# Tiles, banks, sums, masks and first loads of a two-layer network kernel on one Trainium2 core

## The chip, the core and the metric

The kernel runs on one core of a Trainium2 chip. The metric is the device time of one execution in microseconds. Before the change three runs took 2057.19, 2058.51 and 2059.92 us, so the median is 2058.51.

## The reference

The network has two residual layers on a stream of 512 tokens and 2048 features, all in fp32.

- Layer A (HGRN2): an RMS norm, a product with a 2048 x 8192 matrix that gives queries, forget gates, values and an output gate for 16 heads, a gated linear recurrence over the tokens, a norm per head, the gate, a product with a 2048 x 2048 matrix, and the sum with the stream.
- Layer B (forgetting attention): keys, values and forget sums from the stream after layer A, queries and gate, attention with a decay per head, the gate, and again a product with a 2048 x 2048 matrix and the sum.

```python
...
    proj = h @ w_in
...
    o = o.reshape(B, T, D_MODEL) * jax.nn.silu(gate.astype(jnp.float32))
    return x + (o.astype(x.dtype) @ w_out)
```

## The kernel before

Everything is kept with features on the 128 partitions and the 512 tokens along the free axis, so the stream is 16 tiles ("slices", kt) of 128 x 512. An fp32 product is made of three products in a rounded format: each operand is split into a high part h and a low part l, and h·xh, h·xl and l·xh are summed in PSUM. The split of a weight tile is a cast on ScalarE (L435, or L147 where a norm's weight is multiplied in) and a subtraction on VectorE (L436, L148). Weights are read by the SP queue, 512 KB at a time into two buffers `wr` (`Chunks.load`, L190).

An ordinary group (`group`) makes four output tiles in the four PSUM banks `gm0` to `gm3`: 16 slices of 12 matmuls each, 128 x 512 (L237 to L239, with the tokens on the other side L233 to L235). The first one of the program reads the input `x` too, 256 KB a slice (`fetch_x`, L456); `load_x` splits it (L469, L470), feeds the norm's sum of squares (`Norm.add`: ScalarE squares into `z`, GpSimd adds, L350), and does one step of setup for each slice, among them the ten masks of layer A (`mask`: a memset, two selections, a cast, L514 to L523).

The program runs through four phases: layer A ("a"), its output projection ("oa"), layer B ("b"), its output projection ("ob"). Each phase has a pool of its own, which is closed when the next one opens; `mt` takes a tile from the phase's pool, `nt` from a persistent one. In "oa" and "ob" (`out_product`) the first ordinary group makes four of the 16 output tiles, with the splits of its inputs (`y_split`) and the preparation of the sums of inputs (`quick_prep`, tile `tm`) between its slices. Then six seven-product groups (`quick_groups`, `quick`) make two output tiles each, by a scheme of 7 products for 8: 168 matmuls of 128 x 256 (L290 to L292), with sums of weight parts on VectorE (`w_sums`, L156 to L158, tile `wm`) and their split (`w_split_quick`). These groups take the banks `gm` and `mx` in turn; `quick_sum` (L299 to L309) evacuates them. The evacuation of the last of the six in "oa" is deferred (`last_a`) into the third slice of the first group of "b", whose inputs are split by `x1_split`. `x1_done` stores a finished tile of the stream and adds its squares to the next norm. At the end of "a" the gate of the last four heads is made by `gate_evac` (VectorE L381, ScalarE L367 to L384, VectorE L370 and L387) before the inputs of "oa" are complete.

The order of the instructions on each engine is set by a scheduler that simulates the program; each engine then works through its own row of instructions in that order and waits for semaphores. The weights of the split were, before, in tiles of the phase's pool:

```python
    def w_tiles(shape):

        n = 2 if cur["quick"] else 3
        return mt("wh", shape, n, F32R), mt("wl", shape, n, F32R)
```

## Time and profile before

| | |
|---|---|
| runs (us) | 2057.19, 2058.51, 2059.92 |
| profiled execution: time, span (us) | 2057.41, 2055.4 |
| mean granted TensorE clock | 0.987 |
| busy: TensorE, VectorE, ScalarE, GpSimd (us) | 1986.9, 1585.9, 1133.1, 305.6 |
| bytes moved | 195.01 MB |

The profiled execution's own time is 2.0 us over its span. The share of busy time is an average over the stages; where an engine waits is read from the timeline, which gives after each group of instructions the idle time before it and what ended it. A matmul's duration is longer than the distance to the next one's start, since matmuls are pipelined. The granted clock is given as a share of full speed, where 1.0 stands for 2.4 GHz.

### The profile page before, as it was taken

How to read it: one execution, taken by the hardware profiler on the slowest of the kernel's cores; microseconds unless marked ns; L12 is line 12 of the kernel's file. 1: busy time of each engine (PE TensorE's matmuls, PEld its weight loads, DVE VectorE, ACT ScalarE, POOL GpSimd, SP SyncE). 2: the span in 40 equal slices, each digit the busy share in tenths (PEclk: the TensorE clock that was granted, in tenths of full speed). 3: DMA queues.
4: the chain of work that ended last, by engine and by line, in shares of the span. 5: the costliest groups of instructions: out<-in, count | busy, mean ns of one | idle time of the engine just before them, and what ended most of it. 6: DMA issues, size and time to landing. Idle time of an engine off the chain costs nothing.

```text
span 2055.4 us, 28924 instructions
## 1 busy us (share of the span) xinstructions
PE 1986.9 (97%) x10202; PEld 1696.2 (83%) x10202; DVE 1585.9 (77%) x3250; ACT 1133.1 (55%) x2312; POOL 305.6 (15%) x404
## 2 busy tenths in 40 slices
PE   7999999999999999889999999999999999997998
PEld 5888888888888888779987888888888888885898
DVE  8778977989799889688984667666766666687787
ACT  5656655656566466644453555554555556564333
POOL 7303210313133031121110000010001000011000
PEclk9999999999999999989999999999999999998999
DMA  5222222222222222234433233223222322222453
GB/s 170 88 83 74 71 84 81 75 80 83 74 81 72 73 83 73 81 96 151 159 115 95 91 93 97 88 79 101 93 88 92 92 90 90 90 86 72 135 173 103
DMA packets 61408, 195.01 MB, mean 95 GB/s; under 512 B 7872, under 2 KB 8000, under 8 KB 61264
## 3 DMA queue, kind: packets, MB, share of 16 engines
q1 hardware_dynamic: 61120, 193.17, 30.0%
q8 instruction: 80, 1.31, 0.3%
q14 instruction: 64, 0.52, 0.1%
q10 hardware_dynamic: 144, 0.01, 0.0%
HBM read 184.73 MB, written 8.42 MB: 94 GB/s over the span
## 4 chain that ended last, share of the span: by engine, by line
PE 74%; DVE 13%; DMA 4%; issue 3%; ACT 3%; POOL 2%; SPq 0%; DVEq 0%; ACTq 0%; POOLq 0%
PE gm L237 16%; PE gm L239 16%; PE gm L238 16%; PE gm L234 5%; PE gm L233 5%; PE gm L235 5%; DVE wl L436 3%; DMA wr<-in_wa_q 2%; DMA wr<-in_wb_q 2%; PE mx L583 1%; PE mx L581 1%; PE mx L582 1%; DVE ml L436 1%; PE mx L430 1%; PE mx L431 1%
## 5 line engine op out<-in xcount | busy, mean ns | idle before, releaser
L237 PE MATMUL gm<-xh,wh 128*128 128x512 f32 x1664 | 654.2, 393 | 37.6 <-ACT wh L435 36.5
L238 PE MATMUL gm<-xl,wh 128*128 128x512 f32 x1664 | 653.5, 393 | 0.0
L239 PE MATMUL gm<-xh,wl 128*128 128x512 f32 x1664 | 605.8, 393 | 6.0 <-DVE wl L436 5.5
L237 PEld LDWEIGHTS gm<-xh,wh 128*128 128x128 f32 x1664 | 314.7, 189 | 102.9 <-ACT wh L435 37.6
L239 PEld LDWEIGHTS gm<-xh,wl 128*128 128x128 f32 x1664 | 312.4, 189 | 70.3 <-DVE wl L436 7.2
L238 PEld LDWEIGHTS gm<-xl,wh 128*128 128x128 f32 x1664 | 314.7, 189 | 63.5
L435 ACT CAST wh<-wr 128x512 fp32r<-128x512 f32 (+1 forms) x336 | 217.4, 650 | 217.6 <-PE gm L238 114.8
L436 DVE TENSOR_TENSOR wl<-wr,wh 128x512 fp32r<-128x512 f32 (+1 forms) x336 | 257.5, 770 | 75.5 <-ACT wh L435 60.7
L148 DVE SCALAR_TENSOR_TENSOR wl<-wr,v_b_norm_w,wh 128x256 fp32r<-128x256 f32 (+1 forms) x192 | 114.1, 596 | 137.5 <-ACT wh L147 129.2
L147 ACT ACTIVATE wh<-wr,v_b_norm_w 128x256 fp32r<-128x256 f32 (+1 forms) x192 | 111.8, 585 | 185.2 <-PE gm L238 144.0
L234 PE MATMUL gm<-wl,xh 128*128 128x512 f32 x512 | 201.5, 394 | 0.4 <-DVE wl L436 0.4
L235 PE MATMUL gm<-wh,xl 128*128 128x512 f32 x512 | 200.0, 392 | 0.0
L233 PE MATMUL gm<-wh,xh 128*128 128x512 f32 x512 | 183.6, 392 | 0.3 <-DVE q L547 0.2
L147 ACT ACTIVATE wh<-wr,v_kv_norm_w 128x256 fp32r<-128x256 f32 (+1 forms) x192 | 110.3, 574 | 59.4 <-PE gm L235 43.1
L148 DVE SCALAR_TENSOR_TENSOR wl<-wr,v_kv_norm_w,wh 128x256 fp32r<-128x256 f32 (+1 forms) x192 | 112.2, 586 | 35.8 <-ACT wh L147 35.3
L934 POOL TENSOR_SCALAR_AFFINE_SELECT s<-s 128x128 f32<-128x128 f32 x64 | 27.3, 427 | 647.7 <-DVE s L933 647.0
L576 DVE COPY_PREDICATED at<-m,mx 128x128 f32<-128x128 uint8 (+3 forms) x448 | 106.8, 297 | 11.2 <-PE mx L583 10.7
L233 PEld LDWEIGHTS gm<-wh,xh 128*128 128x128 f32 x512 | 96.0, 188 | 20.4 <-ACT wh L435 0.5
L234 PEld LDWEIGHTS gm<-wl,xh 128*128 128x128 f32 x512 | 96.3, 188 | 19.5 <-DVE wl L436 1.0
L235 PEld LDWEIGHTS gm<-wh,xl 128*128 128x128 f32 x512 | 96.3, 188 | 18.4
L435 ACT CAST kh<-k 128x512 fp32r<-128x512 f32 (+1 forms) x96 | 56.5, 588 | 52.3 <-PE mx L582 19.2
L385 POOL TENSOR_TENSOR z<-z,t 128x512 f32<-128x512 f32 x32 | 46.4, 1460 | 230.3 <-ACT t L384 230.3
(217 smaller groups left out, 3890.4 us busy)
## 6 DMA issues: line engine op xcount, KB each, us to landing
wr<-in_wa_qf SPq DMA_DIRECT2D x64, 512.0 KB, 3.5
wr<-in_wb_qk SPq DMA_DIRECT2D x64, 512.0 KB, 3.5
wr<-in_wa_v SPq DMA_DIRECT2D x32, 512.0 KB, 3.5
wr<-in_wa_g SPq DMA_DIRECT2D x32, 512.0 KB, 3.5
wr<-in_wb_v SPq DMA_DIRECT2D x32, 512.0 KB, 3.5
wr<-in_wb_g SPq DMA_DIRECT2D x32, 512.0 KB, 3.5
wr<-in_wa_q SPq DMA_DIRECT2D x24, 512.0 KB, 3.6
wr<-in_wb_q SPq DMA_DIRECT2D x24, 512.0 KB, 3.6
```

Of the source, the lines that this page charges most:

```text
L147: S.activation(h[:, c], r[:, c], AF.Copy, scale=w[:, kt : kt + 1])
L148: V.scalar_tensor_tensor(l[:, c], r[:, c], w[:, kt : kt + 1], rd(h)[:, c], op0=ALU.mult, op1=ALU.subtract)
L233: PE.matmul(banks[j], xh, h, start=f, stop=False)
L234: PE.matmul(banks[j], xh, l, start=False, stop=False)
L235: PE.matmul(banks[j], xl, h, start=False, stop=e)
L237: PE.matmul(banks[j], h[:, c], Xh[kt], start=f, stop=False)
L238: PE.matmul(banks[j], h[:, c], Xl[kt], start=False, stop=False)
L239: PE.matmul(banks[j], l[:, c], Xh[kt], start=False, stop=e)
L385: G.tensor_mul(z, z, l)
L435: S.copy(h, src)
L436: return V.tensor_sub(l, src, rd(h))
L576: V.copy_predicated(out, mv, data)
```

## The change

1. Weight tiles: `w_tiles` is gone. An ordinary split takes three buffers `wh`, `wl` of the persistent pool in all phases; a seven-product split takes two buffers `w7h`, `w7l` of the phase's pool. The scratch tile `t` has three buffers in the output projections and four elsewhere, and the tile of `quick_prep` is one of the two buffers `wm`.
2. Banks: the seven-product groups 0, 2 and 4 take `mx`, the groups 1, 3 and 5 `gm`; before it was the other way round.
3. Norm sums: `Norm.add` adds on VectorE instead of GpSimd, and the call for layer B's norm is moved from `x1_done` (when a tile of the stream is finished) to `x1_split` (when the next phase splits it).
4. Masks: all ten are made in one tile at the start, with one memset, twenty selections and one cast.
5. First loads: the first two weight loads are halved, and each half follows an input tile.

```diff
--- before.py
+++ after.py
@@ -65,7 +65,7 @@
         return t.bitcast(F32)
 
     def tmp():
-        return mt("t", (P, T), 4)
+        return mt("t", (P, T), cur["t"])
 
     def bank():
         return nt("mx", (P, T), 4, pool=ps)
@@ -78,7 +78,7 @@
         if cur:
             cur["ctx"].close()
         cur["ctx"] = c = ExitStack()
-        cur["quick"] = name[0] == "o"
+        cur["t"] = 3 if name[0] == "o" else 4
         cur["sb"] = c.enter_context(tc.tile_pool(name=f"sb{name}", bufs=1, reuse_waits="tile"))
 
     phase("a")
@@ -131,13 +131,8 @@
     load_vec("a_norm_w", S)
 
 
-    def w_tiles(shape):
-
-        n = 2 if cur["quick"] else 3
-        return mt("wh", shape, n, F32R), mt("wl", shape, n, F32R)
-
     def w_split(r, kt, scales):
-        h, l = w_tiles((P, T))
+        h, l = nt("wh", (P, T), 3, F32R), nt("wl", (P, T), 3, F32R)
         if scales is None:
             split(r, h, l)
         else:
@@ -160,7 +155,7 @@
 
     def w_split_quick(r, m):
 
-        h, l = w_tiles((P, 2, 7, P))
+        h, l = mt("w7h", (P, 2, 7, P), 2, F32R), mt("w7l", (P, 2, 7, P), 2, F32R)
         split(r[:, :, 1:4, :], h[:, :, 0:3, :], l[:, :, 0:3, :])
         split(m, h[:, :, 3:7, :], l[:, :, 3:7, :])
         return [(h[:, i, :, :], l[:, i, :, :]) for i in range(2)]
@@ -181,13 +176,18 @@
             for k in range(KT // 4):
                 self.todo.append((ap[k], True, None, 0))
 
-        def load(self):
+        def load(self, between=None):
 
             if not self.todo:
                 return
             ap, quick, scales, kt = self.todo.pop(0)
             r = nt("wr", (P, 2 * T), 2)
-            nc.sync.dma_start(r, ap)
+            if between:
+                nc.sync.dma_start(r[:, :T], ap[:, :T])
+                between()
+                nc.sync.dma_start(r[:, T:], ap[:, T:])
+            else:
+                nc.sync.dma_start(r, ap)
             if quick:
                 self.raw.append((lambda r=r.rearrange("p (a b c) -> p a b c", a=2, c=P): w_split_quick(r, w_sums(r)), 2))
             else:
@@ -250,7 +250,7 @@
 
         k1, k2 = 2 * p, 2 * p + 1
         b11, b12, b21, b22 = y[k1][:, :TN], y[k1][:, TN:], y[k2][:, :TN], y[k2][:, TN:]
-        m = mt("tm", (P, 4, TN), 1)
+        m = mt("wm", (P, 4, TN), 2)
         V.tensor_sub(m[:, 0, :], b12, b11)
         G.tensor_sub(m[:, 2, :], b12, b22)
         V.tensor_sub(m[:, 1, :], b22, m[:, 0, :])
@@ -313,7 +313,7 @@
         for u in range(6):
             k = 4 + 2 * u
             r = [residual(k), residual(k + 1)]
-            banks = [nt(f"gm{j}", (P, T), 1, pool=ps) if u % 2 == 0 else bank() for j in range(4)]
+            banks = [nt(f"gm{j}", (P, T), 1, pool=ps) if u % 2 else bank() for j in range(4)]
             end = quick(banks, prep, lambda *p, k=k, r=r: evac(k, r, p), hold and u == 5)
             if u < 5:
                 end()
@@ -347,7 +347,7 @@
             else:
                 q = nt("z", (P, T), 4)
                 S.activation(q, x, AF.Square)
-                G.tensor_add(self.acc, self.acc, q)
+                V.tensor_add(self.acc, self.acc, q)
             self.n += 1
 
         def finish(self):
@@ -455,11 +455,10 @@
             xs.append(nt(f"y{kt}", (P, T), 1))
             nc.sync.dma_start(xs[kt], io["x"][kt])
 
-    for kt in range(2):
-        fetch_x()
-    wts.load()
     fetch_x()
+    wts.load(fetch_x)
     fetch_x()
+    wts.load(fetch_x)
 
     def load_x(kt):
         fetch_x()
@@ -503,15 +502,19 @@
     setup.append(lower_bounds)
 
 
-    def mask(name, m, d, q0):
-        n = 4 - q0
-        g = P // (4 * m)
-        u = const(name, (P, g * n * m), U8)
-
-        def make():
-            f = tmp()
-            fv = f[:, : g * n * m].rearrange("p (g q r) -> p g q r", g=g, q=n)
-            G.memset(f[:, : g * n * m], 1.0)
+    masks = {}
+    levels = [(1, 0, 0), *((m, d, d) for m in (1, 4, 16) for d in (1, 2, 3))]
+    sizes = [P // 4 * (4 - q0) for _, _, q0 in levels]
+    all_masks = const("masks", (P, sum(sizes)), U8)
+
+    def make_masks():
+        f = mt("e", (P, 4 * T))[:, : sum(sizes)]
+        G.memset(f, 1.0)
+        at = 0
+        for (m, d, q0), size in zip(levels, sizes):
+            n = 4 - q0
+            g = P // (4 * m)
+            fv = f[:, at : at + size].rearrange("p (g q r) -> p g q r", g=g, q=n)
             G.affine_select(
                 out=fv, in_=fv, pattern=[[-4 * m, g], [-m, n], [0, m]], compare_op=ALU.is_ge,
                 fill=0.0, base=m * (d - q0), channel_multiplier=1,
@@ -520,15 +523,11 @@
                 out=fv, in_=fv, pattern=[[4 * m, g], [m, n], [0, m]], compare_op=ALU.is_ge,
                 fill=0.0, base=m * (q0 - d) + m - 1, channel_multiplier=-1,
             )
-            V.tensor_copy(u, f[:, : g * n * m])
-
-        setup.append(make)
-        return u
-
-    masks = {(1, 0): mask("m1_0", 1, 0, 0)}
-    for m in (1, 4, 16):
-        for d in (1, 2, 3):
-            masks[m, d] = mask(f"m{m}_{d}", m, d, d)
+            masks[m, d] = all_masks[:, at : at + size]
+            at += size
+        V.tensor_copy(all_masks, f)
+
+    make_masks()
     ats = [const(f"at{i}", (P, NW, P)) for i in range(2)]
     setup.append(lambda: [V.memset(t, 0.0) for t in ats])
 
@@ -804,7 +803,6 @@
 
     def x1_done(kt):
         nc.sync.dma_start(x1_d[kt], X1[kt])
-        norm1.add(X1[kt])
 
     def out_a_evac():
         res = [res_a(j) for j in range(4)]
@@ -851,6 +849,7 @@
             forget_weights()
         h, l = new_x(kt)
         split(X1[kt], h, l)
+        norm1.add(X1[kt])
         X1[kt] = None
         if kt == KT - 1:
             norm1.finish()
@@ -859,7 +858,7 @@
     wfs = mt("wfs", (P, KT, 48), 1, F32R)
 
     def forget_weights():
-        wf = mt("t", (P, KT, H), 4)
+        wf = mt("t", (P, KT, H), cur["t"])
         nc.sync.dma_start(wf, io["wb_f"])
         V.memset(wfs.bitcast(F32), 0.0)
         V.tensor_mul(wf, wf, view(nk, 0, [[1, KT], [0, H]]))
```

Three places show how the order moves. In all rows a line of the changed kernel has its own line numbers (L143 is the old L148, L186 and L188 are the halves of a load, L532 the old L533).

The SP queue at the start of the program; `y` is an input tile, `wr` a weight buffer. Before:

```order
L456 DMA y_3_84<-in_x 128x512
L456 DMA y_4_86<-in_x 128x512
L190 DMA wr_88<-in_wa_qf 128x1024
L456 DMA y_6_90<-in_x 128x512
L456 DMA y_7_92<-in_x 128x512
L128 DMA v_lb<-in_lb 128x16
```

And now:

```order
L456 DMA y_3_84<-in_x 128x512
L186 DMA wr_86<-in_wa_qf 128x512
L456 DMA y_5_88<-in_x 128x512
L188 DMA wr_86<-in_wa_qf 128x512
L456 DMA y_6_91<-in_x 128x512
L186 DMA wr_93<-in_wa_qf 128x512
L456 DMA y_8_95<-in_x 128x512
L188 DMA wr_93<-in_wa_qf 128x512
L128 DMA v_lb<-in_lb 128x16
```

The first weights come in halves of 128 x 512, the first of them behind one input tile, and the second weight load comes ahead of the small vectors.

ScalarE at the end of phase "a" and the start of "oa"; L367 to L384 are the gate of the last heads, `xh` are input splits, `wh` weight splits. Before, from the last steps of the gate:

```order
L384 ACTIVATE t_9250<-t_9250 128x512
L384 ACTIVATE t_9263<-t_9263 128x512
L384 ACTIVATE t_9276<-t_9276 128x512
L435 CAST xh_1878_9641<-y_1426_7294 128x512
L435 CAST xh_1882_9661<-y_1502_7684 128x512
L435 CAST xh_1890_9694<-y_1619_8290 128x512
L435 CAST wh_9323<-wr_9214 128x512
L435 CAST wh_9327<-wr_9214 128x512
```

And now, from the last split of the group before:

```order
L435 CAST wh_9291<-wr_9148 128x512
L435 CAST wh_9295<-wr_9148 128x512
L367 ACTIVATE t_9205<-z_9203 128x512
L435 CAST wh_9326<-wr_9182 128x512
L367 ACTIVATE t_9218<-z_9216 128x512
L368 ACTIVATE t_9205<-t_9205 128x512
L367 ACTIVATE t_9231<-z_9229 128x512
L368 ACTIVATE t_9218<-t_9218 128x512
L367 ACTIVATE t_9244<-z_9242 128x512
L369 ACTIVATE t_9205<-t_9205 128x512
L368 ACTIVATE t_9231<-t_9231 128x512
```

The first three weight splits of the projection (`wh_9291`, `wh_9295`, `wh_9326`), which came behind the gate, stand ahead of it and in its first steps.

VectorE at the end of the last seven-product group of "oa" and the start of "b"; L436 with `xl` are the next phase's input splits, L350 the norm's sums, L300 to L309 the deferred evacuation. Before, from the last weight split of the projection:

```order
L436 TENSOR_TENSOR wl_11142<-wm_11137,wh_11141 128x2x512
L436 TENSOR_TENSOR xl_2144_11534<-y_2047_10977,xh_2143_11533 128x512
L436 TENSOR_TENSOR xl_2148_11556<-y_2048_10978,xh_2147_11555 128x512
L864 MEMSET wfs_11216 128x768
L148 SCALAR_TENSOR_TENSOR wl_11229<-wr_11168,v_b_norm_w,wh_11228 128x256
L148 SCALAR_TENSOR_TENSOR wl_11229<-wr_11168,v_kv_norm_w,wh_11228 128x256
L148 SCALAR_TENSOR_TENSOR wl_11235<-wr_11168,v_b_norm_w,wh_11234 128x256
L148 SCALAR_TENSOR_TENSOR wl_11235<-wr_11168,v_kv_norm_w,wh_11234 128x256
L148 SCALAR_TENSOR_TENSOR wl_11257<-wr_11222,v_b_norm_w,wh_11256 128x256
L148 SCALAR_TENSOR_TENSOR wl_11257<-wr_11222,v_kv_norm_w,wh_11256 128x256
L300 TENSOR_TENSOR t_11279<-t_11278 128x256
L301 TENSOR_TENSOR t_11278<-t_11279,mx_11003 128x256
```

And now, with two sums more between the last weight split and the first of these rows:

```order
L436 TENSOR_TENSOR xl_2132_11490<-y_2028_10911,xh_2131_11489 128x512
L350 TENSOR_TENSOR rstd_9268<-rstd_9268,z_11362 128x512
L436 TENSOR_TENSOR xl_2137_11515<-y_2029_10912,xh_2136_11514 128x512
L350 TENSOR_TENSOR rstd_9268<-rstd_9268,z_11389 128x512
L350 TENSOR_TENSOR rstd_9268<-rstd_9268,z_11414 128x512
L350 TENSOR_TENSOR rstd_9268<-rstd_9268,z_11441 128x512
L863 MEMSET wfs_11144 128x768
L350 TENSOR_TENSOR rstd_9268<-rstd_9268,z_11466 128x512
L300 TENSOR_TENSOR t_11211<-t_11210 128x256
L350 TENSOR_TENSOR rstd_9268<-rstd_9268,z_11493 128x512
L301 TENSOR_TENSOR t_11210<-t_11211,gm_2036_10931 128x256
L350 TENSOR_TENSOR rstd_9268<-rstd_9268,z_11518 128x512
L302 TENSOR_TENSOR t_11211<-gm_2038_10933,t_11211 128x256
```

Seven of the norm's sums stand in these rows, and the evacuation's last reads of `gm` come behind them; the banks that it read before were `mx`.

## Rows read from the trace of the kernel before

**Rows 1.** The page, part 1: busy us, share of the span, instructions.

```profile
PE 1986.9 (97%) x10202; PEld 1696.2 (83%) x10202; DVE 1585.9 (77%) x3250; ACT 1133.1 (55%) x2312; POOL 305.6 (15%) x404
```

**Rows 2.** The page, part 4, the chain that ended last, by engine.

```profile
PE 74%; DVE 13%; DMA 4%; issue 3%; ACT 3%; POOL 2%; SPq 0%; DVEq 0%; ACTq 0%; POOLq 0%
```

**Rows 3.** Busy time by stretch: length, busy us (count), granted clock.

```profile
core 0: us, PE busy (x) PEld busy (x) DVE busy (x) ACT busy (x) POOL busy (x), PEclk, DMA share, GB/s
864.00:929.00 65.00, 47.73 (x203) 38.71 (x201) 52.18 (x80) 33.08 (x55) 13.34 (x12) 0.89 0.30 89
929.00:1035.50 106.50, 104.24 (x841) 102.70 (x842) 96.06 (x134) 45.67 (x56) 17.20 (x11) 0.99 0.47 149
1035.50:1064.20 28.70, 24.60 (x170) 23.08 (x169) 24.18 (x36) 15.09 (x25) 3.60 (x2) 0.88 0.34 110
1861.00:1924.80 63.80, 46.88 (x195) 37.91 (x193) 49.75 (x79) 33.18 (x56) 12.62 (x12) 0.87 0.30 91
1924.80:2029.00 104.20, 103.59 (x841) 102.65 (x842) 85.62 (x135) 38.84 (x44) 0.00 (x0) 0.98 0.49 160
```

**Rows 4.** Timeline of TensorE at the start; in brackets idle before it.

```profile
7.65 0.80 PE L237 MATMUL gm<-xh,wh 128*128 128x512 f32 x1 [7.65 <-ACT wh L435]
...
36.44 2.07 PE L239 MATMUL gm<-xh,wl 128*128 128x512 f32 x4 [4.14 <-DVE wl L436]
38.31 0.63 PE L237 MATMUL gm<-xh,wh 128*128 128x512 f32 x1
```

**Rows 5.** Timeline of TensorE at the edges of the output projections.

```profile
881.16 0.80 PE L237 MATMUL gm<-xh,wh 128*128 128x512 f32 x1 [14.71 <-ACT wh L435]
...
929.22 0.55 PE L290 MATMUL gm<-xh,wh 128*128 128x256 f32 x1 [2.79 <-DVE y L814]
...
1064.04 0.40 PE L237 MATMUL gm<-xh,wh 128*128 128x512 f32 x1
...
1875.75 0.79 PE L237 MATMUL gm<-xh,wh 128*128 128x512 f32 x1 [14.11 <-ACT wh L435]
...
1924.84 0.36 PE L290 MATMUL gm<-xh,wh 128*128 128x256 f32 x1 [2.84 <-DVE z L1003]
```

**Rows 6.** Groups of GpSimd, 0 to 64 us: count, busy us, mean ns.

```profile
L350 POOL TENSOR_TENSOR rstd<-rstd,z 128x512 f32<-128x512 f32 x15 | 23.6, 1574 | 0.6
L515 POOL TENSOR_SCALAR_AFFINE_SELECT t<-t 128x96 f32<-128x96 f32 (+3 forms) x10 | 7.5, 760 | 0.0
L519 POOL TENSOR_SCALAR_AFFINE_SELECT t<-t 128x96 f32<-128x96 f32 (+3 forms) x10 | 7.3, 742 | 0.0
```

**Rows 7.** Groups of VectorE, 0 to 62 us.

```profile
L436 DVE TENSOR_TENSOR wl<-wr,wh 128x512 fp32r<-128x512 f32 x18 | 16.6, 945 | 11.8 <-ACT wh L435 11.5
L470 DVE SCALAR_TENSOR_TENSOR xl<-y,v_a_norm_w,xh 128x512 fp32r<-128x512 f32 x16 | 16.0, 1013 | 2.8 <-ACT xh L469 2.8
```

**Rows 8.** DMA issues, 0 to 12 us: count, KB each, median us to landing.

```profile
wr<-in_wa_qf SPq DMA_DIRECT2D x3, 512.0 KB, 5.2
```

**Rows 9.** Timeline of ScalarE before the first projection.

```profile
879.97 0.62 ACT L435 CAST xh<-y 128x512 fp32r<-128x512 f32 x1 [1.12 <-DVE y L387]
880.49 1.13 ACT L435 CAST wh<-wr 128x512 fp32r<-128x512 f32 x2
```

**Rows 10.** Timeline of VectorE, 879 to 880 us.

```profile
879.20 0.68 DVE L387 TENSOR_TENSOR y<-y,z 128x512 f32<-128x512 f32 x1
879.80 0.68 DVE L436 TENSOR_TENSOR xl<-y,xh 128x512 fp32r<-128x512 f32 x1
```

**Rows 11.** Groups of VectorE, 929 to 1064 us.

```profile
L156 DVE TENSOR_TENSOR wm<-wr 128x512 f32<-128x512 f32 x22 | 18.4, 837 | 9.9 <-DMA wr<-in_wa_q 9.9
```

**Rows 12.** Groups of VectorE, 1923 to 2049 us.

```profile
L156 DVE TENSOR_TENSOR wm<-wr 128x512 f32<-128x512 f32 x22 | 15.2, 691 | 16.2 <-DMA wr<-in_wb_q 16.1
```

**Rows 13.** Timeline of TensorE in the first projection's last seven-product group.

```profile
1050.63 0.39 PE L292 MATMUL mx<-xh,wl 128*128 128x256 f32 x1 [1.48 <-DVE wl L436]
...
1053.78 0.41 PE L292 MATMUL mx<-th,wl 128*128 128x256 f32 x1
```

## The prediction

> **What bounds the kernel now.** I began with the busy times. TensorE is busy for 1986.9 of 2055.4 us, VectorE for 1585.9 [rows 1]. No part of a saving reaches the end unless TensorE starts a matmul earlier. The chain of waits says the same: 74% of the chain that ended last is TensorE and 13% is VectorE [rows 2]. That leaves about 68 us outside TensorE's busy time, so I looked for where they are. The table by stage [rows 3] shows that they are not spread out. From 864 to 929 us, the ordinary group that opens the first output projection, TensorE is busy for 47.73 of 65 us at a granted clock of 0.89. Its twin in the second projection, 1861 to 1924.8, has 46.88 of 63.8 at 0.87. In the long seven-product stretches TensorE is busy nearly throughout (104.24 of 106.5 and 103.59 of 104.2), except in the last seven-product group of the first projection: 24.60 of 28.7 us at 0.88. The timeline of TensorE then gives the single holes: the start [rows 4] and the stage edges [rows 5].
>
> The chip's level of the clock matters because a hole costs more than its length: behind the hole that ends at 36.44 us a 512-column matmul takes 0.63 us [rows 4], against 0.40 at 1064.04, which waits for nothing [rows 5]; these are the 1.2 and the 2.4 GHz level.
>
> **The sum, part by part.** Against the profiled run's own 2057.4 us (span 2055.4), which is 1.1 us under the median of the runs.
>
> *Start of the program (first loads, masks, sums on VectorE).* The first matmul starts at 7.65 us and waits for ScalarE's cast of the first weights [rows 4], whose 512 KB take 5.2 us to land in this stretch [rows 8]. Now half of them, behind one input tile and not two, are enough for the first cast. The gain lies between 0 and half of 5.2 = 2.6 us; I take 1.8, since the other half and one 256 KB tile no longer stand in front. The SP queue issues two more transfers, but the eight small vectors behind them are needed only by the setup work. Later TensorE waits 4.14 us for a low part of the weights on VectorE, and the six matmuls after it cost 0.63 - 0.40 = 0.23 us more each: 1.4 us [rows 4]. VectorE is late there because GpSimd's fifteen sum additions, 1574 ns each [rows 6], run beside it: its 18 weight parts average 945 ns and its 16 input parts 1013 ns, where an undisturbed operation of that size takes 0.68 [rows 7, 10]. The change moves the additions to VectorE, at 0.68 for each at most: 15 x 0.68 = 10.2 us more work, against (0.945 - 0.68) x 18 + (1.013 - 0.68) x 16 = 10.1 us less inflation and ten small casts that become one. VectorE's load is thus the same, without the burst at one place; I let the 4.1 + 1.4 us go, with 0 as the other end. New is that the mask cast on VectorE stands in its queue behind all twenty selections of GpSimd, 7.5 + 7.3 us [rows 6]; they start at the beginning now, so they end near 3 + 15 = 18 us, when TensorE is at the fifth slice of its group and VectorE has the parts up to there ready. I cost this wait at nothing; if VectorE is held longer, TensorE waits for the sixth slice, up to 3 us. **Start: -7.3 us, from 0 to -10.**
>
> *Start of the first output projection (weight parts in the same tiles in all phases).* TensorE stops for 14.71 us until 881.16 [rows 5]. What ends it is the cast of the first weights at 880.49, which stands on ScalarE behind the whole gating of the group before and behind three casts of the last inputs [rows 9]. The weights are not late; the tiles of the split belonged to the phase's own pool. Now they outlive the phase, and the order rows put three of these casts among or ahead of the gating. TensorE can then start as the four banks come free; the four last inputs are needed only at the twelfth slice. The 14.7 us and the slow matmuls behind them go, but the group then runs into VectorE. Its work in this stretch is 52.18 us [rows 3], two weight parts (1.4 us) of it now before. If it still idles 3.5 us on casts, the first seven-product group begins 54.3 us after 864.0, near 918.3, instead of 929.22 [rows 5]. That is 10.9 us; I take 10, because the sums for that group now share their tiles with the preparation of the inputs and come a little later. The 2.79 us before the group [rows 5], a wait for the evacuation of the banks, goes with the other banks, but only in favour of a wait for VectorE. **-10 us; ends -2 (VectorE keeps all of its 65 - 52.2 = 12.8 us of idle) and -17.5 (14.71 + 2.79).**
>
> *Second output projection.* The same holes, 14.11 and 2.84 us [rows 5], and less work on VectorE, 49.75 us [rows 3]: 1861 + 49.75 - 1.4 + 3.5 = 1912.9 instead of 1924.84. **-11 us; ends -2 and -17.** Its last part stays as it was: after the last matmul comes the same evacuation from other banks.
>
> *Seven-product groups of the first projection.* Eleven of the additions on GpSimd lie beside the first five groups, 17.20 us [rows 3]; the sums of the weights average 837 ns there and 691 in the second projection, where GpSimd does nothing [rows 11, 12]. Without them these five groups should approach the second projection's: 106.5 against 104.2 us [rows 3]. **-2 us, from 0 to -5.**
>
> *End of that projection and start of the next phase.* This is where the change pays. The sixteen squares and fifteen additions are now issued with the splits of the next phase's inputs, so they land in the last seven-product group and right after it. VectorE is late there already: TensorE waits 1.48 us for it and then runs 256-column matmuls at 0.41 us, and the group takes 28.7 us where the five before it take 106.5 / 5 = 21.3 [rows 3, 13]. The additions add 15 x 0.60 = 9.0 us to VectorE (a 512-wide operation starts 0.60 us after the one before [rows 10]) and take back some 2 us of slowing by the two GpSimd additions in the stretch. On top, this group now fills the four banks that the next phase's first group wants, where before there was no hole at the edge (the matmul at 1064.04 waits for nothing [rows 5]). The order rows show ScalarE's copy from the first bank behind the last squares, and VectorE's reads of the others behind the last nine additions: 9 x 0.60 = 5.4 us. VectorE gets 7 us of work more; TensorE has some 2 us of slack from the first three slices that it can take bank by bank. **+5 us; ends -4 (the last group runs as in the second projection, and only the evacuation is waited for) and +12 (all of the additions and the banks' wait in a row).** The Trainium skill, Perfetto Trace Analysis, section Matmuls, says that independent groups of matmuls should go round through different PSUM banks, so that the evacuation of one lies beside the matmuls of the next. By that rule the swap is right at the six-group start and wrong here; the trace of before agrees (2.8 us of wait where the bank was shared, none where it wasn't), and by the rule alone this edge would cost what those cost, 2.8 us, so that the time would come out 2 us lower, near 2031.
>
> *The rest:* the pool of the scratch tiles and the larger count of weight tiles touch no hole that the trace shows; I cost them at nothing, covered by TensorE's own work in the steady groups.
>
> Sum: -7.3 - 10 - 2 + 5 - 11 = **-25.3 us**, 2032.1 for the profiled run and about **2033** for the median.
>
> **Rivals.**
> *VectorE takes the place of what was removed (0.17).* It keeps most of its idle time in both opening groups, because it waits on casts in pairs with TensorE. Then the openings give 2 to 5 us each, the edge costs 8, and the start its 7.3: near 2050. For it: 52.18 busy of 65 us. Against: most of that idle lies in the hole itself.
> *TensorE alone binds (0.15).* Both openings lose their two holes entirely (-17.5 and -17), the edge costs nothing, the rest as above: -7.3 - 34.5 - 3, near 2014. Against it stands VectorE's 52.18 us for a group that TensorE could do in some 44.
> *The early casts don't come (0.06).* The change does not do what it says if the casts wait anyway, for the two load buffers or behind the gating; the 14 us holes stay, and start, seven-product groups and edge give -4.3: near 2054.
> *Slower: the clock falls at the edge (0.05).* Several short holes follow one another in the last seven-product group and at the next phase's start. If TensorE then stays at the 1.2 GHz level through the first group of that phase, its 192 matmuls cost 0.23 us more each, 44 us: near 2077. It decides from 110 matmuls on (110 x 0.23 = 25.3 us, all of the gain). Against it: after 4.14 us of hole the slow level lasted six matmuls [rows 4], and in the last seven-product group the mean stayed at 0.88 [rows 3].
> The forecast has 0.55 (its own range 2022 to 2045). The last 0.02 I leave to the far ends of the terms together.
>
> **The numbers.** A measurement of this kernel tells 0.2%, 4.1 us, from no change: under 2054.4 is faster. The forecast, the first rival and the second lie below that: 0.87. The third rival, with a tail of the first, gives about the same: 0.07. The last, and the far ends together, are slower: 0.06. The range reaches from just above the second rival, whose better half it leaves out, at 2016, to just above the first, 2051; with the third and the last, some 0.18 lies outside.
>
> **What would show it.** Right: first matmul near 5.9 us and no wait over 1 us before 60; no hole over 3 us at 860 to 880 and its twin; a wait of 2 to 6 us for VectorE ahead of the seven-product groups; new waits for banks or VectorE at the next phase's start, of some 5 us with the longer last group; no additions on GpSimd beside these. Wrong: if the opening groups still take over 60 us from the end of the phase before, if the edge costs over 12 us, or if a mask cast holds VectorE past 20 us and TensorE with it.

## The result and the profile after

The changed kernel takes 2028.63 us (median of four runs, 2027.88 to 2030.30), the kernel before 2057.85 in the same comparison. The ratio is 0.986 with a 95% interval of 0.9843 to 0.9877: 1.4% faster, clear of the noise. The profiled execution took 2028.3 us with a span of 2026.6 at a mean granted clock of 0.993 (before 2055.4 at 0.987).

The page of the changed kernel, part 1 (busy time) and part 4 (the chain that ended last), beside [rows 1, 2]:

```profile
PE 1983.9 (98%) x10202; PEld 1696.2 (84%) x10202; DVE 1567.3 (77%) x3271; ACT 1129.9 (56%) x2312; POOL 272.2 (13%) x365
...
PE 77%; DVE 12%; DMA 4%; ACT 3%; issue 2%; POOL 2%; SPq 0%; DVEq 0%; ACTq 0%; POOLq 0%
```

TensorE's busy time is 3 us less than before, and the span 28.8 us less. So nearly all of the gain is holes that closed. VectorE's total fell by 18.6 us although it took over thirty additions, and GpSimd's by 33.4.

Where the time went is read best from six stages, each from the end of the one before to a matmul that both kernels have. The starts of these matmuls come from the timeline of TensorE: the last matmul of the recurrence in the first phase, a sum for a head's norm (`mx<-sl`, L331; 837.71 us before, 828.81 after), the last of the first seven-product group (951.09, 932.73), the last of the fifth (1035.27, 1014.33), the same sum at the end of the phase of layer B (1861.24, 1845.87), the last of the second projection's first seven-product group (1946.43, 1919.10), and the last of all (2049.03, 2020.30).

| stage, us | before | after | change | forecast |
|---|---|---|---|---|
| 1. start, to the end of the recurrence | 837.7 | 828.8 | -8.9 | -7.3 |
| 2. opening of the first projection and its first seven-product group | 113.4 | 103.9 | -9.5 | -10 |
| 3. seven-product groups two to five | 84.2 | 81.6 | -2.6 | -2 |
| 4. last seven-product group, edge, phase of layer B | 826.0 | 831.5 | +5.6 | +5 |
| 5. opening of the second projection and its first seven-product group | 85.2 | 73.2 | -12.0 | -11 |
| 6. the other five groups | 102.6 | 101.2 | -1.4 | 0 |

The holes themselves are on the timeline of TensorE in the changed kernel (start, duration, instruction, in brackets the idle time before it and what ended it):

```profile
5.94 2.08 PE L237 MATMUL gm<-xh,wh 128*128 128x512 f32 x4 [5.94 <-ACT wh L435]
...
32.42 1.19 PE L239 MATMUL gm<-xh,wl 128*128 128x512 f32 x4 [0.86 <-DVE wl L436]
...
869.19 1.19 PE L239 MATMUL gm<-xh,wl 128*128 128x512 f32 x4 [1.64 <-DVE wl L436]
...
908.91 0.58 PE L290 MATMUL mx<-th,w7h 128*128 128x256 f32 x1 [4.06 <-ACT w7h L435]
...
912.29 0.58 PE L292 MATMUL mx<-th,w7l 128*128 128x256 f32 x1 [1.31 <-DVE w7l L436]
...
1037.41 0.58 PE L290 MATMUL gm<-th,w7h 128*128 128x256 f32 x1 [3.39 <-ACT w7h L435]
...
1046.97 0.50 PE L237 MATMUL gm<-xh,wh 128*128 128x512 f32 x1 [1.94 <-ACT t L299]
...
1047.65 0.63 PE L239 MATMUL gm<-xh,wl 128*128 128x512 f32 x1
...
1895.58 0.39 PE L290 MATMUL mx<-th,w7h 128*128 128x256 f32 x1 [2.91 <-ACT w7h L435]
...
1898.58 0.58 PE L292 MATMUL mx<-th,w7l 128*128 128x256 f32 x1 [1.79 <-DVE w7l L436]
```

The first matmul starts 1.71 us earlier than before, and of the wait of 4.14 us near 36 us [rows 4] 0.86 is left. The stop of 14.71 us ahead of the first projection [rows 5] is gone; in its place stands a short wait for a weight part, 1.64 us. New are the waits inside the first seven-product groups, 4.06 and 1.31 us, with their twins in the second projection of 2.91 and 1.79, and those at the next phase's edge: 3.39 us for the weights of the last seven-product group, and 1.94 for ScalarE's copy from the bank, after which the 512-column matmuls take 0.63 us. Before, that edge had no hole.

The busy times by stretch, beside [rows 3] (columns as there):

```profile
core 0: us, PE busy (x) PEld busy (x) DVE busy (x) ACT busy (x) POOL busy (x), PEclk, DMA share, GB/s
857.50:903.60 46.10, 44.16 (x193) 35.68 (x192) 42.39 (x67) 27.51 (x49) 17.54 (x12) 1.00 0.35 103
903.60:932.70 29.10, 23.73 (x168) 23.22 (x167) 20.84 (x34) 9.76 (x13) 0.00 (x0) 0.82 0.47 161
932.70:1014.20 81.50, 81.06 (x673) 80.65 (x672) 68.95 (x109) 32.15 (x36) 0.00 (x0) 1.00 0.49 156
1014.20:1044.80 30.60, 24.48 (x172) 23.17 (x170) 27.89 (x48) 20.38 (x35) 0.00 (x0) 0.89 0.32 108
1846.00:1891.40 45.40, 44.20 (x194) 35.86 (x193) 40.46 (x68) 27.59 (x50) 21.28 (x12) 1.00 0.34 104
```

The first row is the opening group: 44.16 of 46.1 us busy, where before it was 47.73 of 65. The second row is the group that pays: TensorE is busy for 23.73 of 29.1 us at a granted clock of 0.82, where the stretch after it runs at 1.00. In the last seven-product group, fourth row, VectorE is busy for 27.89 of 30.6 us: nearly without a break.

At the start VectorE now works without the slowing. Its groups, 0 to 62 us (count, busy us, mean ns, idle before), beside [rows 7]:

```profile
L436 DVE TENSOR_TENSOR wl<-wr,wh 128x512 fp32r<-128x512 f32 x21 | 14.4, 700 | 9.0 <-ACT wh L435 8.9
L469 DVE SCALAR_TENSOR_TENSOR xl<-y,v_a_norm_w,xh 128x512 fp32r<-128x512 f32 x16 | 11.7, 750 | 2.8 <-ACT xh L468 2.7
L350 DVE TENSOR_TENSOR rstd<-rstd,z 128x512 f32<-128x512 f32 x15 | 10.4, 694 | 0.1
```

The weight parts average 700 ns instead of 945, the input parts 750 instead of 1013, and the fifteen additions take 694 each where GpSimd took 1574 [rows 6].

### The profile page after: what moved, and what is told of

Its sections match the earlier page's. It is cut to its first block, busy times and chain, and to the rows that moved or that the text cites. A ratio compares the mean times of both kernels' runs of the same rounds, so it can differ in the third digit from the quotient of the medians.

```text
span 2026.6 us, 28876 instructions
## 1 busy us (share of the span) xinstructions
PE 1983.9 (98%) x10202; PEld 1696.2 (84%) x10202; DVE 1567.3 (77%) x3271; ACT 1129.9 (56%) x2312; POOL 272.2 (13%) x365
## 3 DMA queue, kind: packets, MB, share of 16 engines
q8 instruction: 80, 1.31, 0.3%
## 4 chain that ended last, share of the span: by engine, by line
PE 77%; DVE 12%; DMA 4%; ACT 3%; issue 2%; POOL 2%; SPq 0%; DVEq 0%; ACTq 0%; POOLq 0%
PE gm L237 15%; PE gm L238 15%; PE gm L239 15%; PE gm L234 5%; PE gm L235 5%; PE gm L233 5%; DMA wr<-in_wa_q 3%; DVE wl L436 2%; PE mx L292 1%; DVE w7l L436 1%; PE mx L582 1%; PE mx L580 1%; PE mx L581 1%; PE mx L291 1%; PE mx L290 1%
## 5 line engine op out<-in xcount | busy, mean ns | idle before, releaser
L239 PE MATMUL gm<-xh,wl 128*128 128x512 f32 x1664 | 613.5, 392 | 4.6 <-DVE wl L436 4.0
L237 PEld LDWEIGHTS gm<-xh,wh 128*128 128x128 f32 x1664 | 313.5, 188 | 73.1 <-ACT wh L435 5.9
L436 DVE TENSOR_TENSOR wl<-wr,wh 128x512 fp32r<-128x512 f32 x288 | 213.1, 744 | 67.3 <-ACT wh L435 59.6
L435 ACT CAST wh<-wr 128x512 fp32r<-128x512 f32 x288 | 177.2, 619 | 125.3 <-PE gm L238 92.3
L143 DVE SCALAR_TENSOR_TENSOR wl<-wr,v_b_norm_w,wh 128x256 fp32r<-128x256 f32 (+1 forms) x192 | 113.1, 591 | 140.0 <-ACT wh L142 133.1
L143 DVE SCALAR_TENSOR_TENSOR wl<-wr,v_kv_norm_w,wh 128x256 fp32r<-128x256 f32 (+1 forms) x192 | 111.2, 581 | 35.8 <-ACT wh L142 35.2
L575 DVE COPY_PREDICATED at<-masks,mx 128x128 f32<-128x128 uint8 (+3 forms) x448 | 107.1, 298 | 11.2 <-PE mx L582 10.7
L435 ACT CAST w7h<-wr 128x768 fp32r<-128x768 f32 x48 | 40.1, 835 | 106.3 <-PE mx L291 57.8
```

What stands on the lines that cost most here:

```text
L143: V.scalar_tensor_tensor(l[:, c], r[:, c], w[:, kt : kt + 1], rd(h)[:, c], op0=ALU.mult, op1=ALU.subtract)
L237: PE.matmul(banks[j], h[:, c], Xh[kt], start=f, stop=False)
L239: PE.matmul(banks[j], l[:, c], Xh[kt], start=False, stop=e)
L435: S.copy(h, src)
L436: return V.tensor_sub(l, src, rd(h))
L575: V.copy_predicated(out, mv, data)
```

## The experiments

Each kernel is the changed kernel with one edit, unless the text says otherwise. The table gives the medians, with the kernel before measured in the same comparison, and the stages of the profiled execution as above.

| kernel | median us | before | ratio, 95% interval | 1 | 2 | 3 | 4 | 5 | 6 |
|---|---|---|---|---|---|---|---|---|---|
| changed kernel | 2028.63 | 2057.85 | 0.986, 0.9843 to 0.9877 | 828.8 | 103.9 | 81.6 | 831.5 | 73.2 | 101.2 |
| tiles_back | 2045.34 | 2058.31 | 0.9936, 0.9921 to 0.9951 | 828.5 | 110.5 | 82.0 | 831.3 | 82.1 | 102.8 |
| banks_back | 2017.03 | 2058.31 | 0.9802, 0.9787 to 0.9816 | 828.5 | 101.9 | 81.5 | 821.6 | 72.7 | 102.8 |
| sums_gpsimd | 2044.51 | 2058.31 | 0.9935, 0.992 to 0.995 | 836.5 | 103.4 | 82.8 | 836.6 | 73.2 | 101.9 |
| sums_early | 2024.47 | 2058.31 | 0.9833, 0.9817 to 0.985 | 828.5 | 103.1 | 82.5 | 827.9 | 72.3 | 102.4 |
| tiles_banks_back | 2043.58 | 2059.10 | 0.9924, 0.9909 to 0.9939 | 828.4 | 110.5 | 81.8 | 827.4 | 81.1 | 104.3 |
| tiles_only | 2034.54 | 2059.10 | 0.9878, 0.9862 to 0.9895 | 838.8 | 102.9 | 85.5 | 825.3 | 72.5 | 103.6 |
| banks_back_sums_early | 2019.34 | 2059.10 | 0.9807, 0.9792 to 0.9822 | 828.8 | 102.6 | 82.0 | 823.7 | 71.9 | 102.7 |
| masks_spread | 2029.88 | 2059.10 | 0.9859, 0.9844 to 0.9873 | 830.9 | 104.0 | 82.2 | 831.7 | 72.9 | 101.6 |
| prep_light | 2020.77 | 2058.48 | 0.9819, 0.9804 to 0.9834 | 828.4 | 97.8 | 82.1 | 831.4 | 70.0 | 101.7 |
| loads_back | 2031.28 | 2058.48 | 0.987, 0.9855 to 0.9885 | 829.7 | 104.1 | 82.1 | 831.6 | 73.1 | 101.2 |
| banks_mixed | 2018.02 | 2058.48 | 0.9804, 0.9787 to 0.982 | 828.6 | 101.9 | 82.7 | 821.3 | 73.0 | 104.6 |

One profile of a stage isn't exact: banks_back and banks_mixed are the same program up to the end of stage 3, and differ there by 1.2 us (81.5 and 82.7). So a difference of a stage below some 1.2 us shows nothing by itself. The lines of the table come from several comparisons, each with its own measurement of the kernel before; where the intervals of two kernels overlap widely, their medians aren't told apart.

### The weight tiles: tiles_back and tiles_only

The first edit puts the weight parts back into tiles of the phase's pool (`w_tiles` as before). The rest of part 1 of the change, the buffers of `t` and the tile of `quick_prep`, stays:

```diff
-        h, l = nt("wh", (P, T), 3, F32R), nt("wl", (P, T), 3, F32R)
+        h, l = w_tiles((P, T))
...
-        h, l = mt("w7h", (P, 2, 7, P), 2, F32R), mt("w7l", (P, 2, 7, P), 2, F32R)
+        h, l = w_tiles((P, 2, 7, P))
```

> The changed kernel with the weight parts in tiles of the phase's pool again, shared by both kinds of split (two buffers in the output projections). Theory (the life of the tiles held the casts back): TensorE's holes of about 14 us ahead of both output projections come back, the wait of 4.1 and 2.9 us for the seven-product weights of the first such group goes, and the time rises by about 9.6 + 12 = 21 us, to some 2050. Rival (the holes went because the banks or the sums were moved): at most one hole of 3 us comes back, and the time rises by under 5 us.

It took 2045.34 us, 16.7 more. The timeline of TensorE in this kernel, at the two openings:

```profile
872.42 0.79 PE L243 MATMUL gm<-xh,wh 128*128 128x512 f32 x1 [15.22 <-ACT wh L441]
...
1866.84 0.79 PE L243 MATMUL gm<-xh,wh 128*128 128x512 f32 x1 [14.11 <-ACT wh L441]
```

Both holes are back with their old lengths (14.71 and 14.11 us before [rows 5]), and the rest of the change does not touch them. The rival is out. The price was 4 us under the expectation: stages 2 and 5 grow by 6.6 and 8.9 us, not 9.6 and 12. The waits inside the first seven-product groups shrink to 0.72 and 0.67 us when TensorE comes later, as expected, so what the tiles save is about the hole less the waits that take its place. But some 3 us of each opening's gain stay with the old tiles; tiles_banks_back below bears on these.

The other way round, the kernel before was given the new tiles, with the rest of part 1, and nothing else but a single tile for the masks, built one by one as before:

```diff
-        h, l = w_tiles((P, T))
+        h, l = nt("wh", (P, T), 3, F32R), nt("wl", (P, T), 3, F32R)
...
-        h, l = w_tiles((P, 2, 7, P))
+        h, l = mt("w7h", (P, 2, 7, P), 2, F32R), mt("w7l", (P, 2, 7, P), 2, F32R)
```

> The kernel before with the new tiles alone (all masks in one tile, which is smaller, but made one by one as before; the sums on GpSimd, the old banks, the old loads). Its order has 29 matmuls of the next phase among the last seven-product group. Theory (the tiles alone make the openings 6.4 and 8.9 us shorter, as their removal cost, and let those 29 matmuls fill some 8 us of waiting): near 2035. Rival (the filling is only worth something after the sums are moved): near 2043.

It took 2034.54 us, as the theory said, but the number is luck: the split is another. Stages 2 and 5 are 10.5 and 12.7 us shorter than before, where the theory had 6.4 and 8.9, and stage 4 only 0.7, where it had some 8. So the two openings account for all of it, and the 29 matmuls brought next to nothing here: they start at 1050.89 us, behind the waits of that group. The longest of these, and the first of the 29:

```profile
1042.21 0.39 PE L287 MATMUL mx<-xh,w7l 128*128 128x256 f32 x1 [1.48 <-DVE w7l L431]
...
1050.89 0.40 PE L232 MATMUL gm<-xh,wh 128*128 128x512 f32 x1
```

Part 1 by itself is worth 24.6 us, and the tiles taken from the changed kernel cost 16.7; the parts overlap, and no share of the 29 us is theirs alone.

### The banks: banks_back, tiles_banks_back and banks_mixed

```diff
-            banks = [nt(f"gm{j}", (P, T), 1, pool=ps) if u % 2 else bank() for j in range(4)]
+            banks = [nt(f"gm{j}", (P, T), 1, pool=ps) if u % 2 == 0 else bank() for j in range(4)]
```

> The changed kernel with the seven-product groups' banks in the old turn. Theory (VectorE sets the start of the first seven-product group, so its banks do not matter there): at most 1 us more at each of the two openings; the 1.94 us of wait for the bank at the start of the next phase goes, with some of the slow matmuls behind it: 2025 to 2029. Rival (the swap earns its 2.8 us at each opening, as a rotation of banks should): 2 x 2.8 us more, 3 less at the edge, near 2031.

It took 2017.03 us: 11.6 less than the changed kernel, and far outside what either theory allowed. The openings were as the theory said: stages 2 and 5 do not grow (101.9 and 72.7 us against 103.9 and 73.2), although TensorE waits for the evacuation of the shared banks again, 5.08 and 4.82 us. The gain is in stage 4, 9.9 us. The timeline of TensorE at the first opening, in the last seven-product group, and the first matmul behind it:

```profile
908.55 0.58 PE L290 MATMUL gm<-xh,w7h 128*128 128x256 f32 x1 [5.08 <-DVE y L812]
...
1026.04 0.39 PE L292 MATMUL mx<-xh,w7l 128*128 128x256 f32 x1 [1.21 <-DVE w7l L436]
...
1030.98 0.40 PE L237 MATMUL gm<-xh,wh 128*128 128x512 f32 x1
1031.21 0.40 PE L238 MATMUL gm<-xl,wh 128*128 128x512 f32 x1
...
1033.59 0.73 PE L239 MATMUL gm<-xh,wl 128*128 128x512 f32 x2 [0.26 <-DVE wl L143]
...
1043.59 0.63 PE L239 MATMUL gm<-xh,wl 128*128 128x512 f32 x2
```

Among the 256-column matmuls of this group (banks `mx`) stand 512-column matmuls into `gm`: they are the next phase's first group. Counted over the group there are 32 of them, at 0.23 us from one to the next some 7.3 us of work, where the changed kernel waits. The stretch of the group, with the columns of the table of stretches:

```profile
1012.00:1043.60 31.60, 28.85 (x203) 26.48 (x202) 28.58 (x51) 21.77 (x40) 0.00 (x0) 1.00 0.34 116
```

TensorE is busy for 28.85 of 31.6 us at a clock of 1.00; in the changed kernel it was 24.48 of 30.6 at 0.89. The waits of 3.39 us in the group and of 1.94 us behind it are both gone. In the changed kernel this filling is impossible: the last seven-product group itself holds the four `gm` banks that the next phase's group writes.

Whether the old banks gain by themselves was asked by setting both back, tiles and banks:

> The changed kernel with both the weight tiles and the turn of the banks as before. In the run with the old banks alone, 32 matmuls of the next phase's first group stood among those of the last seven-product group, where TensorE had waited for VectorE; in this kernel's order none do. Theory (the old banks gain only together with tiles that outlive the phase, because only then can the next phase start early): 2041 to 2046, against 2045.3 with the old tiles alone. Rival (the old turn of the banks gains by itself, since the next phase's banks are free): 11.6 us less, near 2034.

It took 2043.58 us, against 2045.34 with the old tiles alone. The theory holds: without the tiles that outlive the phase the banks give 1.8 us in the whole, which the intervals don't tell from nothing. In stage 4 they give some 4 (831.3 to 827.4): a wait of 2.43 us for the bank gives way to one of 1.12 for a weight cast, and the group before it is 1 us shorter. The other 6 of the 10 us in stage 4 come only where both are there. The kernel before had the banks for it, and not the tiles; the changed kernel has the tiles, and gave the banks away.

With both set back, the openings are still shorter than before, 110.5 and 81.1 us against 113.4 and 85.2, and the wait for the shared banks ahead of the first seven-product group is 0.57 us in each, where it was 2.79 and 2.84 [rows 5]. What is left of the change in the second opening is the rest of part 1, the buffers of `t` and the tile of `quick_prep`, which is thus the likely cause; no run has them alone.

The last run of this group keeps the new turn in the second projection, behind which no phase follows:

```diff
-            banks = [nt(f"gm{j}", (P, T), 1, pool=ps) if u % 2 else bank() for j in range(4)]
+            banks = [nt(f"gm{j}", (P, T), 1, pool=ps) if (u % 2 == 0) == hold else bank() for j in range(4)]
```

> The changed kernel with the old turn of the banks in the first output projection, where the next phase can start early, and the new turn in the second, where nothing follows. Theory (in the second projection the turn moves the wait from the banks to VectorE and back, under 1.5 us): 2015 to 2018, against 2017.0 with the old turn in both. Rival (the new turn saves its bank wait there): 2014 or less.

It took 2018.02 us, as the theory said, and can't be told from banks_back. In the openings the turn of the banks is worth nothing.

### The sums: sums_gpsimd, sums_early and banks_back_sums_early

```diff
-                V.tensor_add(self.acc, self.acc, q)
+                G.tensor_add(self.acc, self.acc, q)
```

> The changed kernel with the additions of both norms on GpSimd again, at their new places. Theory (at the start GpSimd's additions slow VectorE): VectorE's weight parts in the first 60 us average over 0.9 us again, a hole of 3 to 5 us for them comes back and the start loses 5 to 7 us; at the end of the first output projection VectorE has 9 us less work but is slowed by the same additions, within 2 us: near 2035. Rival (the masks' casts and selections were what held VectorE at the start): the start stays within 1 us, and the edge gains: 2024 to 2028.

It took 2044.51 us, 15.9 more. Stage 1 loses 7.7 us, a little more than the theory said, and stage 4 another 5.1, where it had within 2; so the total lies 9.5 us over the theory's. VectorE's groups, 0 to 62 us, in this kernel:

```profile
L469 DVE SCALAR_TENSOR_TENSOR xl<-y,v_a_norm_w,xh 128x512 fp32r<-128x512 f32 x16 | 19.7, 1263 | 4.0 <-ACT xh L468 4.0
L436 DVE TENSOR_TENSOR wl<-wr,wh 128x512 fp32r<-128x512 f32 x18 | 19.4, 1090 | 9.4 <-ACT wh L435 9.2
```

They are slower than in the kernel before (1013 and 945 ns [rows 7]). In the last seven-product group, 1022.6 to 1062 us, where 13 additions of GpSimd stand now:

```profile
L151 DVE TENSOR_TENSOR wm<-wr 128x512 f32<-128x512 f32 x2 | 2.4, 1224 | 2.6 <-DMA wr<-in_wa_q 2.6
```

The two sums of weight parts there take 1224 ns, against 691 where GpSimd does nothing [rows 12]. The holes of TensorE that belong to it, one at the start and two in the last seven-product group:

```profile
34.76 1.65 PE L239 MATMUL gm<-xh,wl 128*128 128x512 f32 x3 [4.29 <-DVE wl L436]
...
1040.15 0.54 PE L292 MATMUL gm<-xh,w7l 128*128 128x256 f32 x1 [4.92 <-DVE w7l L436]
...
1057.64 0.58 PE L292 MATMUL gm<-th,w7l 128*128 128x256 f32 x1 [5.51 <-DVE w7l L436]
```

This shows that the move to VectorE earns its place at the start, and that the burst at the edge would have been worse on GpSimd.

The other half of the move, the later place, is undone by

```diff
         nc.sync.dma_start(x1_d[kt], X1[kt])
+        norm1.add(X1[kt])
...
         split(X1[kt], h, l)
-        norm1.add(X1[kt])
```

> The changed kernel with the sums of the second norm issued where a tile of the stream is finished, as before, but on VectorE. Theory (the additions come in a burst where VectorE is late): the last seven-product group of the first projection and the edge behind it lose their 5.6 us nearly whole, the first five groups take 1 to 2 us more: near 2025. Rival (VectorE is short of time in the whole projection, and moving its work only moves the wait): the first seven-product group takes 3 us more, the total stays within 1 us of 2028.6.

It took 2024.47 us, 4.2 less; the intervals overlap at their ends, and the stages bear it out. Stage 4 falls by 3.6 us; stage 3 rises by 0.9, which is within the scatter. But the gain isn't where the theory put it. The last seven-product group holds two of the additions instead of eight, and still takes 30.3 us against 30.4, with 6.3 us of waits against 6.1. What goes is the edge behind it: the wait of 1.94 us for the bank, and the ten slow matmuls after it. The last matmul of the group and the next phase's first ones follow one another at once, although the group ends in the same `gm` banks as in the changed kernel:

```profile
1044.30 0.41 PE L292 MATMUL gm<-th,w7l 128*128 128x256 f32 x1
1044.51 0.61 PE L237 MATMUL gm<-xh,wh 128*128 128x512 f32 x1
1044.94 0.42 PE L238 MATMUL gm<-xl,wh 128*128 128x512 f32 x1
1045.19 0.40 PE L239 MATMUL gm<-xh,wl 128*128 128x512 f32 x1
```

So the new turn of the banks alone makes no wait there; it takes the late additions too, and the wait then costs 3.6 us with what stands behind it. The other 1.8 of the 5.6 us that stage 4 lost lie inside the last seven-product group (30.4 us against 28.7 before). The late sums don't make it longer: with them, but with the old tiles and the old turn, it takes 28.7 us again (tiles_banks_back).

With the old banks as well:

> The changed kernel with the old turn of the banks, and with the second norm's sums issued where a tile of the stream is finished, on VectorE. Theory (the matmuls of the next phase cover the burst of sums already): 2016 to 2018, no more than 1 us from the run with the old banks alone. Rival (the two gains add up): 2017.0 - 4.2, near 2013.

It took 2019.34 us, 2.3 more than banks_back, but the intervals of the two overlap nearly whole (0.9807 and 0.9802), so a loss isn't shown in the total. The rival is out: the two gains don't add up. With the old turn the early place takes nothing from stage 4 (823.7 against 821.6 us), and with the early place the old turn takes some 4 us from it (827.9 to 823.7), not 9.9. Where the next phase's matmuls fill the waits, the burst costs nothing; why stage 4 is 2 us longer with the early place was not tried.

### The start: loads_back and masks_spread

```diff
+    for kt in range(2):
+        fetch_x()
+    wts.load()
     fetch_x()
-    wts.load(fetch_x)
     fetch_x()
-    wts.load(fetch_x)
```

> The changed kernel with the first two weight loads whole and in their old place. Theory (the halves only bring the first matmul forward): the first matmul at 7.5 to 7.8 us and the whole 1.5 to 2 us later, 2030 to 2031. Rival (the first group is held later on by other waits that absorb the lead): first matmul later, mid of the first phase within 0.5 us, 2028 to 2029.

It took 2031.28 us, 2.7 more, with intervals that overlap. The first matmul started at 6.64 us, not 7.5 as the theory had it, and the end of the recurrence came 0.9 us later. So the direction is the theory's, but the size isn't shown. Profiles of kernels with the new loads start between 5.30 and 5.94 us, and this one and the kernel before, which issue the first transfers in the same order, start at 6.64 and 7.65. Of the 1.71 us of earlier start, 0.7 separate this run from the changed kernel.

The other edit makes the masks in the steps of the setup again, each with a memset, two selections and a cast:

```diff
...
-    make_masks()
...
+    at = 0
+    for level, size in zip(levels, sizes):
+        masks[level[0], level[1]] = all_masks[:, at : at + size]
+        setup.append(lambda level=level, at=at, size=size: make_mask(*level, at, size))
+        at += size
```

> The changed kernel with the masks made one by one in the steps of the setup, each with its own cast, in one tile. Theory (GpSimd's selections do not slow VectorE, only its additions did, and they are gone): within 1 us of 2028.6 in the whole, and the mid of the first phase within 1 us. Rival (the ten casts in VectorE's row, each behind its selections, hold it at the start): a hole of over 1 us for weight parts in the first 45 us, and 2 to 4 us more.

It took 2029.88 us, 1.2 more, which the intervals don't tell from nothing. Stage 1 of its profile is 2.1 us longer, and TensorE's timeline has two small holes there, the second of which stands in the changed kernel too (0.86 us at 32.42):

```profile
30.02 0.50 PE L237 MATMUL gm<-xh,wh 128*128 128x512 f32 x1 [0.96 <-ACT wh L435]
32.93 1.20 PE L239 MATMUL gm<-xh,wl 128*128 128x512 f32 x4 [0.80 <-DVE wl L436]
```

The first is the rival's, a hole for a weight part, but below 1 us; the theory's 1 us for the mid of the phase is exceeded too. The masks at once are worth some 2 us in stage 1 by the one profile, and nothing that shows in the whole. The selections slow VectorE little: in the first 62 us, which hold all twenty of them, its weight parts average 700 ns in the changed kernel and 690 in this one, where they averaged 945 with GpSimd's additions beside them [rows 7].

### The openings: prep_light

What sets the start of the first seven-product groups was asked by leaving work out: the low part of the prepared sums of inputs isn't computed, and the high part stands in its place.

```diff
-        tl = mt(f"tl{p}", (P, 3, TN), 1, F32R)
...
-        split(m[:, 1:4, :], th, tl)
-        return th, tl
+        S.copy(th, m[:, 1:4, :])
+        return th, th
```

> The changed kernel without the low part of the prepared sums of inputs: the high part is used in its place, so eight subtractions of VectorE (0.96 us each) are left out in each opening group of the output projections, and TensorE's work is the same. Theory (VectorE sets when the first seven-product groups flow): in each opening the end of the first seven-product group comes 3 to 6 us earlier and its waits for the seven-product weights shrink; 2017 to 2023 in the whole. Rival (ScalarE's casts or the weight loads set it): no opening gains over 1 us; 2027 to 2029.

It took 2020.77 us. Stages 2 and 5 are 6.1 and 3.2 us shorter, the others the same within 0.5. The wait of 4.06 us becomes

```profile
911.92 0.39 PE L289 MATMUL mx<-th,w7h 128*128 128x256 f32 x1 [1.90 <-ACT w7h L434]
```

and the wait for the low part behind it is gone. So VectorE's work bounds the openings now, in the main: 7.7 us of it left out give back 6.1 and 3.2 us. In the rows the wait is ended by ScalarE's cast `w7h`, but ScalarE waits in its turn. Its timeline in the changed kernel:

```profile
905.62 0.83 ACT L435 CAST w7h<-wr 128x768 fp32r<-128x768 f32 x1 [1.95 <-DMA wr<-in_wa_q]
...
907.81 1.04 ACT L435 CAST w7h<-wm 128x1024 fp32r<-128x1024 f32 x1 [1.05 <-DVE wm L153]
```

The second of the two casts, at whose end TensorE goes on, waits 1.05 us for the last sum `wm` (L153) on VectorE; but the first waits 1.95 us for its weights to land, and what holds that load back was not tried.

## Why the prediction was right

2028.6 us against 2033, inside the range and near the forecast's middle. Step by step:

- **Start, -7.3 forecast, -8.9 measured.** The terms were right: the first matmul 1.71 us earlier (1.8 forecast), the 4.1 us hole and its slow matmuls nearly gone. What I left out were two smaller waits of the kernel before, 0.52 us near 25 us and 0.82 near 28, which went too. The slow matmuls behind the 4.1 us hole were ten and not six, a term of about 2 us instead of 1.4 (the rows are below). That GpSimd's additions were the main cause is shown: put back, they cost stage 1 7.7 us (sums_gpsimd). The masks and the loads, put back one at a time, cost it 2.1 and 0.9; together that is more than 8.9, so the three overlap or single profiles scatter. The mask cast, costed at nothing, cost nothing: it ran at 17.91 us, and TensorE has no wait over 0.2 us between its first matmul and 32.42.
- **First opening, -10 forecast, -9.5 measured; second, -11 and -12.0.** The stops went, the tiles were their cause (tiles_back), and VectorE took their place as the main bound (prep_light). The step that was off is where it shows: I put the first seven-product group at 918.3 us with VectorE's work ahead of it. It began at 903.61, which is 912.5 on the clock of before, since stage 1 is 8.9 us shorter: 5.8 us sooner. The wait came inside it, with slow matmuls, and that group lasts 29.1 us instead of the 21.9 of before. That VectorE's work bounds the end of the group was counted; that the two errors leave -9.5 is in part luck. Nor is all of it the tiles': with tiles and banks set back, 2.9 and 4.1 us of the two gains remain (tiles_banks_back), and the likely source, the rest of part 1, I had costed at nothing.
- **Groups two to five, -2 forecast for five, -2.6 measured for four.** In sums_gpsimd the additions came later too, on GpSimd, and these four groups took 82.8 us; so a part of the gain may be that the additions stand elsewhere, but a scatter of 1.2 us doesn't split 2.6.
- **Edge, +5 forecast, +5.6 measured: right in its size, partly by luck, and wrong in what it could have been.** I charged VectorE's extra work and the wait for the banks. The extra work did not lengthen the last seven-product group (30.4 us with eight of the additions, 30.3 with two); it came out behind the group, as the wait of 1.94 us for the bank and its slow matmuls, 3.6 us in all (sums_early), by way of ScalarE, whose rows stand below. I also took the kernel before as the best that this edge can do, with "no hole at the edge". But the swap's real price is 9.9 us in stage 4: with the old turn the next phase's matmuls would have filled the waits. I listed the tiles that outlive the phase and the banks as separate parts, and did not ask what the two do together.
- **The rule weighed there.** The Trainium skill, Perfetto Trace Analysis, section Matmuls, on rotating independent groups through PSUM banks, as the prediction applied it, spoke against the swap at this edge. The runs agree with its direction. The price that I drew from it, 2.8 us, was that of an evacuation alone; the measured 9.9 us include the matmuls that could not be brought forward, and with the sums early, where no evacuation is waited for, the swap still costs some 4 us. At the openings, where I took the swap for right by it, the swap gained nothing (103.9 us against 101.9 with the old turn).
- **The rivals.** That VectorE takes the place of what was removed happened, and is in the forecast's own terms; it took some 5 us in each opening, where the rival had all of the gain but 2 to 5. TensorE alone didn't bind: the openings lost 9.5 and 12.0 us of the 17.5 and 17 that this rival had. The casts did come early. That the clock stays low at the edge did not happen: the 512-column matmuls at 0.63 us lasted from 1047.65 to 1050.21 us, and soon after it was 0.39 again.

In the kernel before, the slow matmuls behind the hole that ends at 36.44 us [rows 4] last up to this one, and the fast level follows:

```profile
40.44 0.63 PE L238 MATMUL gm<-xl,wh 128*128 128x512 f32 x1
...
41.72 0.40 PE L237 MATMUL gm<-xh,wh 128*128 128x512 f32 x1
```

ScalarE's timeline at the next phase's edge shows the chain that the order rows had shown ahead of the run, squares that wait for VectorE's additions to free their tiles, and the copy from the bank behind them:

```profile
1043.87 0.63 ACT L349 ACTIVATE z<-y 128x512 f32<-128x512 f32 x1 [0.37 <-DVE rstd L350]
1045.02 0.63 ACT L349 ACTIVATE z<-y 128x512 f32<-128x512 f32 x1 [0.52 <-DVE rstd L350]
1045.81 0.63 ACT L349 ACTIVATE z<-y 128x512 f32<-128x512 f32 x1 [0.17 <-DVE rstd L350]
1046.35 0.57 ACT L299 COPY t<-gm 128x512 f32<-128x512 f32 x1
```

## What to carry to other kernels

Ask of a stage edge not only what waits there, but what the next stage could do in the waits of the last one: that needs tiles and accumulation banks that are both free of the stage that ends, and a change that gives one and takes the other shows nothing of this gain. Nor are both enough: in tiles_only they were there, and the next stage's matmuls came behind the waits and gained 0.7 us. Here the turn of the banks that left a hole of 5 us at the openings was the faster one, because the openings were bound mainly by VectorE anyway. An engine's idle time ahead of a hole is worth filling only down to the next engine's bound; leaving out a part of that engine's work tells in one run where that is.

The fastest version found is the changed kernel with the old turn of the banks: 2017.03 us, ratio to the kernel before 0.9802 (0.9787 to 0.9816).

## What was not expected of the hardware

GpSimd's two-input additions slow VectorE's two-input operations beside them: with them at the start VectorE's input parts took 1263 ns on average (sums_gpsimd), without them 750. Of the weight parts in that run, the four that lay beside additions for most of their time took 1744 to 1785 ns each, and the seven with nothing on GpSimd beside them 678 to 693. GpSimd's selections, which have one input, did far less: in the changed kernel five weight parts beside selections took 691 to 878 ns, 729 on average, and the sixteen with nothing beside them 691.
